# Splitting both plain up-projection weight groups early, and moving the norm's squares and its spreading into the first scheme stretch

## The chip, the cores and the metric

The kernel runs on one core of one Trainium2 chip. The metric is the device time of one execution in microseconds (us). Three runs of the kernel before took 1836.43, 1838.71 and 1839.90 us; the median is 1838.71 us. The engines are called as in the profile: PE multiplies matrices, DVE is the vector engine, ACT the engine of activations, POOL the general one, and SP issues most of the loads.

## What is computed

Two batches of tokens (512 and 256, held side by side as 768 columns) pass through two encoder layers with shared weights. The layers differ in their attention; both end in the same MLP, and this is where the change lies:

```python
for layer in range(DEPTH):
    ...
    h = rmsnorm(x, ln_mlp[layer])
    x = x + jnp.square(jax.nn.relu(h @ w_up[layer])) @ w_down[layer]
return rmsnorm(x, ln_f)
```

`w_up` is 1024 by 4096, `w_down` 4096 by 1024. The root of the mean square is one number for each token, so it can be multiplied in after the up-projection: the kernel multiplies `x` times the gain with `w_up` first and applies the factor `R` to the result.

## The kernel before

Activations lie transposed: eight tiles `x[k]` of 128 features by 768 tokens. Each fp32 operand of a product is cut into a rounded part (`whi`, `c` first half) and a remainder (`wlo`, `c` second half), and three matmuls stand for one exact one: hi·hi, hi·lo and lo·hi. ACT makes the rounded part by a copy, DVE the remainder by a subtraction. For a weight tile this is `wsplit` (lines 76 to 81): ACT's `whi<-wraw` at line 80 and DVE's `wlo<-wraw,whi` at line 81. There are three buffers for loaded weights (`wraw`), four each for `whi` and `wlo`.

The MLP of a layer (`mlp`, line 798) makes the up-projection in 16 stretches of 256 output columns, over two halves of the tokens (A and B, 384 each) and two halves of the features.

- The first two stretches are **plain**: four products of 24 matmuls each, 96 in all, from operands `c0` to `c3` that are ready when the attention's output projection ends. Each needs two weight tiles of 1024 columns, split whole.
- The other 14 are **scheme** stretches (`mp` from 2): seven products of 12 matmuls, 84 in all, of the kind of Strassen's and Winograd's. They need four more operands, `c4` to `c7`, and four weight tiles each: one loaded tile as it is (products 1 and 4), two tiles of sums `s` (6 and 5; 7 and 3), made by four POOL additions at line 866, and half a loaded tile (product 2). In the rows of an engine the products stand in the order 1, 3, 2, 6, 4, 7, 5.
- `second()` (line 822) makes `c4` to `c7`: for each of four pairs of feature tiles one ACT copy (line 828), four DVE combinations `t<-x,gains,t` (line 815), and for each of the four results an ACT copy and a DVE subtraction (`c<-t`, line 116, and `c<-t,c`, line 117).
- The norm: `nm.add(x[k])` (line 140) squares a tile on ACT (`sq<-x`, line 147) and adds it to `acc` on DVE (line 152). The squares share nine buffers with the eight tiles `x`, so one square is made, added and freed before the next. `nm.rstd()` sums `acc` over the partitions on PE (`ss`, line 161), then DVE (`ms`, line 164) and POOL (`rt`, line 166) make the factor; `nm.spread` copies it over all partitions on PE (`pb`, line 180) and DVE (`R<-pb`, line 182).
- `finish(z)` (line 893) applies relu and `R` on DVE (`z<-z,R`, line 894), squares on ACT (line 896) and writes the stretch to DRAM (`H<-z`, ACT's queue, line 898). The stretches' results `z` and the temporary `t` of `second()` share three buffers.

In the code before, the first plain stretch comes first, then `second()`, then all eight `nm.add`, then the second plain stretch with its loads and splits, then `rstd`, `spread` and `finish` of both, then the scheme stretches. A scheduler decides the final order on each engine: it moves instructions ahead of others of the same engine where it expects a gain, so the code's order is only its starting point. Within an engine the final order is fixed, and a waiting instruction holds up all that stand behind it.

Of the kernel before, what the change touches and what calls it, by code (L numbers as in the profile page):

```python
# [19 lines left out]
KD = D // P  # L20
# [17 lines left out]
def kernel(ctx: ExitStack, tc: tile.TileContext, a: dict, y: bass.AP):  # L38
# [22 lines left out]
    def ps_tile(tag, name):  # L61
        return psum.tile([P, 512], F32, tag=tag, name=name, bufs=BANKS[tag])
# [4 lines left out]
    def wload(src, width, pieces=1):  # L67

        off = woff.get(src, 0)
        woff[src] = off + P * width  # L70
        raw = wpool.tile([P, 1024], F32, tag="wraw", name="wraw", bufs=3)[:, :width]
        view = a[src][off : off + P * width].rearrange("(p w) -> p w", w=width)
        w = width // pieces
        return raw, [lambda s=slice(i * w, (i + 1) * w): nc.sync.dma_start(raw[:, s], view[:, s]) for i in range(pieces)]

    def wsplit(hi, lo, raw, dve=False):
        if dve:
            nc.vector.tensor_copy(hi, raw)
        else:
            nc.scalar.activation(hi, raw, AF.Copy)  # L80
        nc.vector.tensor_tensor(out=lo, in0=raw, in1=hi.bitcast(F32), op=ALU.subtract)  # L81

    def whilo(width):
        return (wpool.tile([P, 1024], F32R, tag="whi", name="whi", bufs=4)[:, :width],
                wpool.tile([P, 1024], F32R, tag="wlo", name="wlo", bufs=4)[:, :width])
# [43 lines left out]
    def gcol(g, k):  # L129
        return gains[:, g, k : k + 1]  # L130
# [667 lines left out]
    def mlp(layer, src, o, x, es):  # L798
# [7 lines left out]
        nm = Norm(sq)  # L806
# [3 lines left out]
        def put(pool, c, j, src, gain=None):  # L810
            t = comb[c, j] = pool.tile([P, 2, HT], F32R, tag=f"c{c}", name=f"c{c}", bufs=4)
            halve(t[:, 0], t[:, 1], src, gain)

        def stt(out, x_, s, y_, op):
            nc.vector.scalar_tensor_tensor(out=out, in0=x_, scalar=s, in1=y_, op0=ALU.mult, op1=op)
# [6 lines left out]
        def second():  # L822

            ts = []
            for j in range(4):
                xa, xb = x[j], x[j + 4]
                t = up.tile([P, 4, HT], F32, tag="z", name="t", bufs=3)
                nc.scalar.activation(t[:, 0], xa[:, A], AF.Copy, scale=gcol(g, j))
                stt(t[:, 1], xa[:, B], gcol(g, j), t[:, 0], ALU.subtract)
                stt(t[:, 2], xb[:, A], gcol(5 + layer, j + 4), t[:, 1], ALU.subtract)  # L830
                put(g2, 6, j, t[:, 2])
                stt(t[:, 3], xb[:, B], gcol(g, j + 4), t[:, 2], ALU.add)
                put(g2, 4, j, t[:, 3])
                stt(t[:, 0], xb[:, A], gcol(g, j + 4), t[:, 0], ALU.subtract)
                put(g2, 7, j, t[:, 0])
                put(g2, 5, j, t[:, 1])
# [6 lines left out]
        def weights(plain=False):  # L843


            raws = []
            for _ in range(2):
                raw, loads = wload("w_up", 1024)
                loads[0]()
                raws.append(raw)  # L850
            a11, a22, a12, a21 = (r[:, i * 512 : (i + 1) * 512] for r in raws for i in range(2))
            if plain:
                out = {}
                for t, ij in zip(raws, (((0, 0), (1, 1)), ((0, 1), (1, 0)))):
                    hi, lo = whilo(1024)
                    wsplit(hi, lo, t)
                    for i, b in enumerate(ij):
                        out[b] = (hi, lo), i * 512
                return out
            sa, sb = (up.tile([P, 1024], F32, tag="s", name="s", bufs=3) for _ in range(2))  # L860
            s2, s1, s3, s4 = (r[:, i * 512 : (i + 1) * 512] for r in (sa, sb) for i in range(2))
            out = {}
            for ps_, t in (((1, 4), raws[0]), ((6, 5), sa), ((7, 3), sb), ((2,), raws[1])):
                if t is sa:
                    for d_, x_, y_ in ((s1, a21, a22), (s2, s1, a11), (s3, a11, a21), (s4, a12, s2)):
                        nc.gpsimd.tensor_tensor(out=d_, in0=x_, in1=y_, op=ALU.add)  # L866
                w = 512 * len(ps_)
                hi, lo = whilo(w)
                wsplit(hi, lo, t[:, :w])
                for i, p in enumerate(ps_):  # L870
                    out[p] = (hi, lo), i * 512
            return out

        def product(ps, ws, cs):

            n = len(cs)
            for q, ((part, base), c) in enumerate(zip(ws, cs)):
                for k in range(4):
                    t = comb[c, k]
                    for i, (a_, b_) in enumerate(((0, 0), (0, 1), (1, 0))):  # L880
                        nc.tensor.matmul(ps, part[a_][:, base + k * P : base + (k + 1) * P], t[:, b_],  # L881
                                         start=q + k + i == 0, stop=q == n - 1 and k == 3 and i == 2)
            return ps

        def bank(n):
            return ps_tile("mm" if n in (6, 7, 3) else "at", "up")[:, :HT]

        def add(out, x_, y_, op=ALU.add):
            nc.vector.tensor_tensor(out=out, in0=x_, in1=y_, op=op)  # L889

        R, H, wait = [], [], []

        def finish(z):
            nc.vector.scalar_tensor_tensor(out=z, in0=z, scalar=0.0, in1=R[0][:, None, :].broadcast_to([P, 2, NT]),
                                           op0=ALU.max, op1=ALU.mult)
            nc.scalar.activation(z, z, AF.Square)
            H.append(dram.tile([P, 2, NT], F32, name=f"H{layer}_{len(H)}"))
            nc.scalar.dma_start(H[-1], z)

        def ztile():  # L900
            return up.tile([P, 4, HT], F32, tag="z", name="z", bufs=3).rearrange("p (i n) t -> p i (n t)", n=2)


        for fp in range(2):
            w = weights(True)
            z = ztile()
            for i in range(2):
                for n, (c, sl) in enumerate((((1, 2), B), ((0, 3), A))):
                    ps = product(bank(6 * n), [w[i, 0], w[i, 1]], c)
                    nc.scalar.activation(z[:, i, sl], ps, AF.Copy)  # L910
            wait.append(z)
            if fp == 0:
                second()
                for k in range(KD):
                    nm.add(x[k])
        R.append(nm.spread(nm.rstd()))
        while wait:
            finish(wait.pop(0))

        hs = []  # L920

        def read(pool, f):

            hr = pa_.tile([P, 2, NT], F32, tag="hr", name="hr", bufs=2)
            nc.gpsimd.dma_start(hr, H[f // 2])  # L925
            for i in range(2):
                hp = pool.tile([P, 2, NT], F32R, tag="hp", name="hp")
                halve(hp[:, 0], hp[:, 1], hr[:, i])
                hs.append((hp[:, 0], hp[:, 1]))

        for mp in range(2, FF // 256):
            w = weights()
            z = ztile()
            z12, z11, z22, z21 = z[:, 0, A], z[:, 0, B], z[:, 1, A], z[:, 1, B]
            one = lambda n: product(bank(n), [w[n]], [n])
            nc.scalar.activation(z11, one(1), AF.Copy)
            p3, p2 = one(3), one(2)
            if mp == FF // 256 - 1:

                g1s.close()  # L940
                pa_ = g1s.enter_context(tc.tile_pool(name=f"dna{layer}", bufs=4, reuse_waits="tile"))
                read(pa_, 0)
                read(pa_, 2)
            add(z12, one(6), z11)
            add(z11, p2, z11)
            p4 = one(4)
            add(z22, one(7), z12)
            add(z21, p4, z22, ALU.subtract)
            p5 = one(5)
            nc.vector.scalar_tensor_tensor(out=z22, in0=p5, scalar=-1.0, in1=z22, op0=ALU.mult, op1=ALU.subtract)  # L950
            add(z12, p5, z12)
            add(z12, p3, z12)
            finish(z)
        g2s.close()

# [33 lines left out]
    o, x, es = even_attention()  # L989
    es.close()  # L990
    hs_, xs, nm, spill = mlp(0, "w_out_e", o, x, hs_)
    sg = cpool.tile([P, 1], F32, name="sg")
    nc.scalar.dma_start(sg, a["subln"])
    nc.vector.tensor_scalar(sg, sg, 1.0 - LAM_INIT, None, op0=ALU.mult)
    o, x, es = odd_attention(xs, nm, sg, spill)
    es.close()
    mlp(1, "w_out_o", o, x, hs_)


# [129 lines left out]
```

## Time and profile before

| what | value |
|---|---|
| median of three runs | 1838.71 us (1836.43 to 1839.90) |
| span of the profiled execution, first to last instruction | 1832.9 us |
| PE busy | 1777.7 us (97%) |
| DVE, ACT, POOL busy | 1118.5, 764.7, 360.4 us |
| PE's matmuls of the up-projections (line 881), both layers | 2736 |
| up-projection of the first layer | from 373.4 us |
| up-projection of the second layer | from 1290.5 us |

The page gives no time of the profiled execution beyond its span; the median of the three runs is 5.8 us above that span, which is what lies around the first and the last instruction and the difference between executions. In a row of the timeline the columns are the start, the duration, the engine, the line, the operation, what it writes and reads, its shape and how many equal ones follow each other; in square brackets stand the idle time before it and what ended it. Durations of DVE rows contain some 0.08 us that overlap with the next row, so the distance of two starts is the better price.

### The profile page before, as it was taken

To read this page: it belongs to the slowest core of one execution; us is meant where nothing else is said; L and a number is where in the kernel's file an instruction comes from. 1 tells how busy PE (TensorE), PEld (TensorE's weight loads), DVE (VectorE), ACT (ScalarE), POOL (GpSimd) and SP (SyncE) were. 2 spreads that over 40 slices of the span, in tenths; PEclk is the share of its full clock that TensorE was granted. 3 is DMA by queue.
4 is the path that set the end of the run, shared out by engine and by line. 5 is a ranking of instruction groups with operands and counts; after the bars stand their busy time and mean duration, and the time that the engine had idled before them with its cause. 6 is when DMAs were issued, how large, how long until landed. Compare 5 with 4: busy or idle time off the path is not lost.

```text
span 1832.9 us, 28509 instructions
## 1 busy us (share of the span) xinstructions
PE 1777.7 (97%) x11358; PEld 1627.8 (89%) x11358; DVE 1118.5 (61%) x2083; ACT 764.7 (42%) x1485; POOL 360.4 (20%) x366
## 2 busy tenths in 40 slices
PE   7999999989999999999999999999799999999997
PEld 6878888879999988888999999988799999888877
DVE  7778646596666734325366776775956667343255
ACT  6665534353433412213235555554534334122143
POOL 2421000014544200000022222220145442000002
PEclk9999999989999999999999999999899999999999
DMA  5011223313333543323311110122133336433233
GB/s 176 32 33 47 66 74 111 106 35 110 121 135 124 198 136 127 127 69 114 99 48 46 47 47 21 53 67 92 35 104 126 136 123 197 136 127 127 70 99 114
DMA packets 50019, 176.70 MB, mean 96 GB/s; under 512 B 5856, under 2 KB 8672, under 8 KB 49888
## 3 DMA queue, kind: packets, MB, share of 16 engines
q1 hardware_dynamic: 38656, 121.91, 21.1%
q0 software_dynamic: 4608, 25.17, 4.1%
q10 hardware_dynamic: 6624, 27.81, 3.8%
q8 instruction: 89, 1.46, 0.3%
q14 instruction: 42, 0.34, 0.1%
HBM read 142.63 MB, written 31.46 MB: 95 GB/s over the span
## 4 chain that ended last, share of the span: by engine, by line
PE 79%; issue 7%; DVE 7%; DMA 3%; ACT 2%; POOL 1%; DVEq 0%; SPq 0%; ACTq 0%; POOLq 0%
PE up L881 25%; PE dna L204 11%; PE dqk L192 7%; PE dnb L204 6%; PE opa L204 5%; PE dvp L192 4%; PE fin L786 3%; PE opb L204 2%; DMA hr<-H 2%; PE npa L204 2%; PE ds L270 2%; PE dpv L713 2%; PE vp L192 1%; PE qp L192 1%; PE npv L598 1%
## 5 line engine op out<-in xcount | busy, mean ns | idle before, releaser
L881 PE MATMUL up<-c,whi 128*128 128x384 f32 x1824 | 469.5, 339 | 0.0
L881 PEld LDWEIGHTS up<-c,whi 128*128 128x128 f32 x1824 | 333.3, 190 | 0.1
L204 PE MATMUL dna<-hp,whi 128*128 128x512 f32 x896 | 331.5, 393 | 1.1 <-DVE hp L117 1.1
L80 ACT ACTIVATE whi<-wraw 128x1024 fp32r<-128x1024 f32 (+2 forms) x200 | 193.3, 967 | 325.2 <-PE dnb L204 223.8
L881 PE MATMUL up<-c,wlo 128*128 128x384 f32 x912 | 308.8, 340 | 17.8 <-DVE wlo L81 17.8
L81 DVE TENSOR_TENSOR wlo<-wraw,whi 128x1024 fp32r<-128x1024 f32 (+2 forms) x204 | 227.5, 1116 | 98.1 <-ACT whi L80 97.9
L204 PE MATMUL dnb<-hp,whi 128*128 128x256 f32 x896 | 250.3, 283 | 0.0
L204 PEld LDWEIGHTS dna<-hp,whi 128*128 128x128 f32 x896 | 168.0, 188 | 41.4 <-DVE hp L117 2.1
L881 PEld LDWEIGHTS up<-c,wlo 128*128 128x128 f32 x912 | 173.0, 190 | 18.5 <-DVE wlo L81 18.4
L866 POOL TENSOR_TENSOR s<-wraw 128x512 f32<-128x512 f32 x56 | 90.9, 1643 | 450.6 <-ACT c L116 217.3
L204 PE MATMUL dna<-hp,wlo 128*128 128x512 f32 x448 | 177.0, 395 | 0.0
L204 PEld LDWEIGHTS dnb<-hp,whi 128*128 128x128 f32 x896 | 167.2, 188 | 0.3
L889 DVE TENSOR_TENSOR z<-up,z 128x384 f32<-128x384 f32 x168 | 92.8, 552 | 105.5 <-PE up L881 103.7
L976 DVE TENSOR_TENSOR x<-dna,x 128x512 f32<-128x512 f32 x56 | 38.7, 691 | 166.1 <-PE dna L204 166.0
L204 PE MATMUL dnb<-hp,wlo 128*128 128x256 f32 x448 | 126.6, 283 | 0.0
L192 PE MATMUL dqk<-whi,xh 128*128 128x256 f32 x384 | 114.7, 299 | 0.0
L192 PE MATMUL dqk<-whi,xl 128*128 128x256 f32 x384 | 107.4, 280 | 0.0
L192 PE MATMUL dqk<-wlo,xh 128*128 128x256 f32 x384 | 107.2, 279 | 0.0
L925 POOL DMA_DIRECT2D hr<-H x32 | 17.5, 548 | 431.4 <-DVE hp L117 395.2
L204 PEld LDWEIGHTS dna<-hp,wlo 128*128 128x128 f32 x448 | 84.2, 188 | 18.7
L80 ACT ACTIVATE whi<-s 128x1024 fp32r<-128x1024 f32 x56 | 59.6, 1064 | 95.5 <-PE up L881 95.5
L698 ACT ACTIVATE de<-ds,m 128x512 f32<-128x512 f32 (+1 forms) x96 | 58.3, 612 | 81.1 <-DVE m L696 81.1
(214 smaller groups left out, 3870.2 us busy)
## 6 DMA issues: line engine op xcount, KB each, us to landing
wraw<-in_w_down_dram SPq DMA_DIRECT2D x72, 512.0 KB, 3.6
wraw<-in_w_up_dram SPq DMA_DIRECT2D x64, 512.0 KB, 3.5
H<-z ACTq DMA_DIRECT2D x32, 768.0 KB, 3.3
hr<-H POOLq DMA_DIRECT2D x32, 768.0 KB, 5.8
wraw<-in_w_in_o_dram SPq DMA_DIRECT2D x24, 512.0 KB, 3.6
wraw<-in_w_in_e_dram SPq DMA_DIRECT2D x16, 512.0 KB, 3.6
x<-in_xT_dram SPq DMA_DIRECT2D x16, 384.0 KB, 5.6
nbias<-in_bias_dram SPq DMA_DIRECT2D x20, 256.0 KB, 3.5
```

Source lines behind the costliest of these rows:

```text
L80: nc.scalar.activation(hi, raw, AF.Copy)
L81: nc.vector.tensor_tensor(out=lo, in0=raw, in1=hi.bitcast(F32), op=ALU.subtract)
L192: nc.tensor.matmul(ps[:, :256], st[:, tk], col(k, part, 0, 256), start=(k == 0 and i == 0), stop=(k == KD - 1 and i == 2))
L204: nc.tensor.matmul(ps[:, : e - s], w, mv[:, s:e], start=(k == 0 and i == 0), stop=(k == nk - 1 and i == 2))
L270: nc.tensor.matmul(out[h], q(a_, hp, qs), k(b_, hp, ks), start=i == 0, stop=i == 2)
L698: nc.scalar.activation(e, s, AF.Exp, bias=m, scale=1.0, accum_out=l2[:, c : c + 1])
L713: nc.tensor.matmul(pv, pt[:, i * P : (i + 1) * P], v[:, k0 // P + i, vc], start=(i == 0), stop=(i == nk - 1))
L786: nc.tensor.matmul(ps, lhs(k, part), mv[:, sl], start=(k == 0 and j == 0), stop=(k == GF - 1 and j == 2))
L866: nc.gpsimd.tensor_tensor(out=d_, in0=x_, in1=y_, op=ALU.add)
L881: nc.tensor.matmul(ps, part[a_][:, base + k * P : base + (k + 1) * P], t[:, b_], start=q + k + i == 0, stop=q == n - 1 and k == 3 and i == 2)
L889: nc.vector.tensor_tensor(out=out, in0=x_, in1=y_, op=op)
L976: evac_halves(pa, pb, lambda ps, s: nc.vector.tensor_tensor(out=xm[:, s], in0=ps, in1=xm[:, s], op=ALU.add))
```

## The change

Both plain stretches' weights are loaded and split ahead of everything else (`both`), the plain stretch itself becomes a function, and `second()` stands between the two. The norm's eight squares and additions move into the first scheme stretch (`mp == 2`), ahead of its first evacuation; `rstd` follows three products later, and `spread` and the `finish` of both plain stretches stand at the end of that stretch, directly ahead of its own `finish`. No instruction of arithmetic is added or removed.

```diff
-        for fp in range(2):
-            w = weights(True)
+        def plain(w):
             z = ztile()
             for i in range(2):
                 for n, (c, sl) in enumerate((((1, 2), B), ((0, 3), A))):
                     ps = product(bank(6 * n), [w[i, 0], w[i, 1]], c)
                     nc.scalar.activation(z[:, i, sl], ps, AF.Copy)
             wait.append(z)
-            if fp == 0:
-                second()
-                for k in range(KD):
-                    nm.add(x[k])
-        R.append(nm.spread(nm.rstd()))
-        while wait:
-            finish(wait.pop(0))
+
+        both = [weights(True) for _ in range(2)]
+        plain(both[0])
+        second()
+        plain(both[1])
...
             one = lambda n: product(bank(n), [w[n]], [n])
+            if mp == 2:
+                for k in range(KD):
+                    nm.add(x[k])
             nc.scalar.activation(z11, one(1), AF.Copy)
             p3, p2 = one(3), one(2)
+            if mp == 2:
+                rt = nm.rstd()
...
             add(z12, p3, z12)
+            if mp == 2:
+                R.append(nm.spread(rt))
+                while wait:
+                    finish(wait.pop(0))
             finish(z)
```

What the scheduler makes of it is seen in the order of instructions on the engines. First DVE in the first layer, where the operands of the plain stretches are complete (`c_4521` is the last of them), a minus for before and a plus for the change:

```order
 L120 SCALAR_TENSOR_TENSOR c_4521<-x_4319,gains,c_4521 128x384
-L152 TENSOR_TENSOR acc<-acc,sq 128x768
-L81 TENSOR_TENSOR wlo<-wraw,whi 128x1024
-L152 TENSOR_TENSOR acc<-acc,sq 128x768
+L81 TENSOR_TENSOR wlo<-wraw,whi 128x1024 x2
 L815 SCALAR_TENSOR_TENSOR t<-x_3718,gains,t 128x384
 L815 SCALAR_TENSOR_TENSOR t<-x_3916,gains,t 128x384
 L815 SCALAR_TENSOR_TENSOR t<-x_3832,gains,t 128x384 x3
```

The remainders of both tiles of the second plain stretch now stand ahead of `second()`; before, only the first of them did, and two additions of the norm beside it.

Second, DVE behind the last operand of `second()`. Before, in the first layer:

```order
L117 TENSOR_TENSOR c_4717<-t,c_4717 128x384
L152 TENSOR_TENSOR acc<-acc,sq 128x768
L81 TENSOR_TENSOR wlo<-wraw,whi 128x1024
L152 TENSOR_TENSOR acc<-acc,sq 128x768
L81 TENSOR_TENSOR wlo<-wraw,whi 128x1024
L152 TENSOR_TENSOR acc<-acc,sq 128x768
L81 TENSOR_TENSOR wlo<-s,whi 128x1024 x2
L164 TENSOR_SCALAR ms<-ss 128x6
L81 TENSOR_TENSOR wlo<-wraw,whi 128x512
```

With the change, in the first layer:

```order
L117 TENSOR_TENSOR c_4729<-t,c_4729 128x384
L81 TENSOR_TENSOR wlo<-wraw,whi 128x1024
L81 TENSOR_TENSOR wlo<-s,whi 128x1024
L152 TENSOR_TENSOR acc<-acc,sq 128x768 x4
L81 TENSOR_TENSOR wlo<-s,whi 128x1024
L152 TENSOR_TENSOR acc<-acc,sq 128x768
L81 TENSOR_TENSOR wlo<-wraw,whi 128x512
L152 TENSOR_TENSOR acc<-acc,sq 128x768
L164 TENSOR_SCALAR ms<-ss 128x6
```

With the change, in the second layer, from the last fifth of `second()` on:

```order
L81 TENSOR_TENSOR wlo<-s,whi 128x1024
L815 SCALAR_TENSOR_TENSOR t<-x_14064,gains,t 128x384 x3
L117 TENSOR_TENSOR c_14463<-t,c_14463 128x384
L117 TENSOR_TENSOR c_14471<-t,c_14471 128x384
L117 TENSOR_TENSOR c_14467<-t,c_14467 128x384
L117 TENSOR_TENSOR c_14474<-t,c_14474 128x384
L152 TENSOR_TENSOR acc<-acc,sq 128x768 x4
L81 TENSOR_TENSOR wlo<-s,whi 128x1024
L152 TENSOR_TENSOR acc<-acc,sq 128x768
L81 TENSOR_TENSOR wlo<-wraw,whi 128x512
L152 TENSOR_TENSOR acc<-acc,sq 128x768 x2
```

Before, the first `wlo<-wraw,whi` of the block belongs to the second plain stretch, and the second, the two of `s` and the half tile to the first scheme stretch. With the change all remainders of the block belong to the first scheme stretch: its first loaded tile, the sum tile of products 6 and 5, then four additions of the norm, and only then the sum tile of products 7 and 3. In the second layer the first two of these stand inside `second()`, and seven additions stand behind it, where the first layer has six.

Third, PE around the norm's two small groups in the first layer (`c_4383` is an operand of product 3, `c_4374` of product 1, `c_4664` of product 6, `c_4518` of product 2, `c_4729` of product 5). Before:

```order
L881 MATMUL up<-c_4521,wlo 128x384
L161 MATMUL ss<-ones,acc 128x2 x6
L881 MATMUL up<-c_4383,whi 128x384 x2
L881 MATMUL up<-c_4383,wlo 128x384
L180 MATMUL pb<-ident,rt 128x128 x6
L881 MATMUL up<-c_4374,whi 128x384 x2
```

With the change, around the sum:

```order
L881 MATMUL up<-c_4474,wlo 128x384
L881 MATMUL up<-c_4518,whi 128x384 x2
L881 MATMUL up<-c_4518,wlo 128x384
L161 MATMUL ss<-ones,acc 128x2 x6
L881 MATMUL up<-c_4664,whi 128x384 x2
```

And around the spreading:

```order
L881 MATMUL up<-c_4729,whi 128x384 x2
L881 MATMUL up<-c_4729,wlo 128x384
L180 MATMUL pb<-ident,rt 128x128 x6
L881 MATMUL up<-c_4374,whi 128x384 x2
L881 MATMUL up<-c_4374,wlo 128x384
```

Before, only three matmuls stood between the sum over the partitions and the spreading; now four whole products (6, 4, 7 and 5) do.

## Prediction

> **What bounds the kernel now.** I read the page first, then PE's waits, then the timeline of the two places where it waits longest, and last the chain behind them.
>
> ```profile
> span 1832.9 us, 28509 instructions
> PE 1777.7 (97%) x11358; PEld 1627.8 (89%) x11358; DVE 1118.5 (61%) x2083; ACT 764.7 (42%) x1485; POOL 360.4 (20%) x366
> ```
>
> PE is busy 97% of the span, so a change that leaves the matmuls as they are can win only what is left: idle time, and time in which matmuls run slowly. PE's list of waits says where the idle time is.
>
> ```profile
> PE up L881 <- DVE wlo L81: 17.8, 2, 9.4
> PE pb L180 <- POOL rt L166: 4.3, 4, 1.4
> ```
>
> 17.8 us lie in two waits, one in each layer's up-projection, and some more in front of the norm's spreading. The timeline of PE shows both places, first layer and then second.
>
> ```profile
> 373.44 0.51 PE L881 MATMUL up<-c,whi 128*128 128x384 f32 x2
> 373.79 0.34 PE L881 MATMUL up<-c,wlo 128*128 128x384 f32 x1
> ...
> 404.54 0.69 PE L881 MATMUL up<-c,wlo 128*128 128x384 f32 x1 [8.41 <-DVE wlo L81]
> 405.03 0.84 PE L881 MATMUL up<-c,whi 128*128 128x384 f32 x2
> ...
> 408.23 0.58 PE L881 MATMUL up<-c,whi 128*128 128x384 f32 x2
> ...
> 421.07 2.11 PE L180 MATMUL pb<-ident,rt 128*128 128x128 f32 x12 [1.42 <-POOL rt L166]
> 422.83 0.99 PE L881 MATMUL up<-c,whi 128*128 128x384 f32 x2
> ...
> 425.66 0.51 PE L881 MATMUL up<-c,whi 128*128 128x384 f32 x2
> ...
> 1290.46 0.51 PE L881 MATMUL up<-c,whi 128*128 128x384 f32 x2
> ...
> 1322.52 0.69 PE L881 MATMUL up<-c,wlo 128*128 128x384 f32 x1 [9.38 <-DVE wlo L81]
> ...
> 1326.72 0.34 PE L881 MATMUL up<-c,wlo 128*128 128x384 f32 x1
> ...
> 1339.15 1.60 PE L180 MATMUL pb<-ident,rt 128*128 128x128 f32 x12 [1.43 <-POOL rt L166]
> ```
>
> Two starts from 373.44 to 373.79 give 0.175 us for a matmul. After the wait it is slower: 11 matmuls stand between 404.54 and 408.23, which is 3.69 us instead of 1.93. The window of the wait shows why.
>
> ```profile
> 396.20:404.50 8.30, 0.00 (x0) 0.00 (x0) 8.30 (x16) 4.72 (x9) 0.00 (x0) 0.62 0.00 0
> ```
>
> The last but two columns are the granted clock: 0.62 in the idle stretch, and DVE's 8.30 us say that DVE was busy throughout. The chain shows with what.
>
> ```profile
> 384.26 2.95 DVE c L117 x2
> 387.21 3.67 DVE t L815 x3
> 390.88 1.88 DVE c L117 x4
> ...
> 393.29 0.87 DVE acc L152
> 394.15 1.59 DVE t L815 x3
> ...
> 403.35 1.15 DVE wlo L81
> ```
>
> DVE makes the scheme's operands and the norm's sums, and the remainder that the second plain stretch needs comes last. PE waits for an order, not for work.
>
> **What the change removes.** The order on the engines shows both remainders of the second plain stretch ahead of `second()`. DVE had the end of the plain operands some 4 us after PE's start and needs 1.15 us for each, so they are there by about 380, and PE asks for them at 373.44 + 96·0.175 = 390.2. That wait goes, with the slow matmuls behind it: 8.41 + 1.76 us in the first layer; in the second 9.38 us and 13 matmuls from 1322.52 to 1326.72, 4.20 us instead of 2.28, so 1.92. The wait for `rt` goes too, since four products (8.4 us) now stand between sum and spreading, where DVE and POOL needed 3.3 us: 1.42 us and 9 slow matmuls from 422.83 to 425.66 (2.83 instead of 1.58, so 1.25) in the first layer, 1.43 in the second. **Removed: 12.84 + 12.73 = 25.6 us.** The small matmuls of sum and spreading stay as many as they were.
>
> **What it adds: a wait at product 3.** The first scheme stretch begins 192 matmuls after the start, product 3 is the second in PE's rows, and it needs the sum tile of products 7 and 3. On DVE this remainder now stands behind `second()`, the loaded tile, the other sum tile and four additions of the norm, and the additions go at the pace of squares that share one free buffer:
>
> ```profile
> 402.40 0.95 DVE L152 TENSOR_TENSOR acc<-acc,sq 128x768 f32<-128x768 f32 x1
> ...
> 404.41 0.95 DVE L152 TENSOR_TENSOR acc<-acc,sq 128x768 f32<-128x768 f32 x1
> ...
> 406.41 0.94 DVE L152 TENSOR_TENSOR acc<-acc,sq 128x768 f32<-128x768 f32 x1
> ```
>
> One addition each 2.0 us. First layer: before, `second()` ended at 402.40 with two additions in it; now one is in it, so 402.40 − 0.87 = 401.5. Two remainders: 403.8. Additions start at 403.8, 405.8, 407.8 and 409.8; ACT ends the fourth square at 409.8, then rounds the sum tile (1.06 us); the remainder ends at 410.8 + 1.2 = 412.0. PE is at product 3 after 204 matmuls, at 409.1, and after two rounded ones, at 409.5, it wants the remainder: a wait of 2.5 us. Second layer: `second()` ended at 1320.39, two additions leave it and two remainders enter it, so 1320.39 − 1.74 + 2.3 = 1320.95, the sum tile is ready 8.2 us later at 1329.15, PE is there at 1290.46 + 35.7 + 0.35 = 1326.5: 2.6 us.
>
> ```profile
> 1320.39 0.94 DVE L152 TENSOR_TENSOR acc<-acc,sq 128x768 f32<-128x768 f32 x1
> ```
>
> **And POOL stretches DVE there.** Beside POOL's additions DVE's small operations take 1.2 to 1.5 us instead of 0.5 (384.26 and 387.21 in the chain: five in 6.6 us instead of 2.5).
>
> ```profile
> 383.85 2.94 POOL L866 TENSOR_TENSOR s<-wraw 128x512 f32<-128x512 f32 x2 [191.18 <-ACT c L116]
> 386.76 1.60 POOL L866 TENSOR_TENSOR s<-s,wraw 128x512 f32<-128x512 f32 x1
> 388.44 1.50 POOL L866 TENSOR_TENSOR s<-wraw,s 128x512 f32<-128x512 f32 x1
> ...
> 410.94 2.54 POOL L866 TENSOR_TENSOR s<-wraw 128x512 f32<-128x512 f32 x2 [21.01 <-DMA wraw<-in_w_up_dram]
> ```
>
> ```profile
> 405.28 1.21 DVE L81 TENSOR_TENSOR wlo<-wraw,whi 128x1024 fp32r<-128x1024 f32 x1
> ```
>
> The next stretch's additions begin 4.5 us after the first loaded tile's remainder (ending 406.4) frees a buffer. Now this remainder ends at 402.7, so POOL runs from 407.2 to about 412.5: over the third and fourth addition and the remainder, 0.8 us each as the rows above have it, 2.3 us. In the second layer it ends at 1312.4 within `second()`, POOL runs from 1317 on over operations that follow each other without a gap, and the whole 4.1 us is lost. **Waits at product 3: 2.5 + 2.3 = 4.8 and 2.6 + 4.1 = 6.7 us**, from 2.5 and 2.6 without POOL to 6.6 and 7.8 with its four operations in full. The page SBUF — State Buffer of the Trainium skill (section Who interferes with whom) says that a DVE instruction with two SBUF inputs and a GpSimd one that reads SBUF exclude each other, so that the later one blocks fully. By that the second layer would lose POOL's 5.2 us (four operations of 1.3) and the time would come out 1.1 us later; the rows above, 4.1 us for the five, agree in kind.
>
> Slow matmuls follow again: rows have 1.76 and 1.92 us behind waits of 8 to 9 us, 1.25 us behind the spreading in the first layer and none in the second, so 0 to 1.9; I take 1.3 and 1.6. The page TensorE: Matmul & The Clock Gate (Part 1) has the clock halved only after an idle window of about 3.4 us; the 0.62 row agrees, and by that waits of 2.5 us would cost no slow matmul.
>
> **What it moves to the third and fourth scheme blocks.** Three `finish` now follow each other on DVE, and the second scheme stretch's `z` needs the buffer of the first plain one.
>
> ```profile
> 422.35 0.69 DVE L182 COPY R<-pb 128x512 f32<-128x512 f32 x1 [2.53 <-PE pb L180]
> 423.21 0.42 DVE L182 COPY R<-pb 128x256 f32<-128x256 f32 x1 [0.17 <-PE pb L180]
> 423.67 3.43 DVE L894 SCALAR_TENSOR_TENSOR z<-z,R 128x1536 f32<-128x1536 f32 x2
> ...
> 432.24 1.15 DVE L889 TENSOR_TENSOR z<-up,z 128x384 f32<-128x384 f32 x2 [5.14 <-PE up L881]
> ```
>
> ```profile
> 426.78 1.47 ACT L896 ACTIVATE z<-z 128x1536 f32<-128x1536 f32 x1
> ```
>
> ```profile
> H<-z ACTq DMA_DIRECT2D x32, 768.0 KB, 3.3
> ```
>
> Count from the end X of product 2. The sum (1.25) and four products reach X + 9.7, the spreading X + 11.5, and PE ends the second scheme stretch at X + 26.2. DVE has the first copy of `R` at X + 11.7, an addition, the second copy and the last half remainder at X + 13.4, or 15.8 if POOL stretches the three remainders there by 0.8 each. The first `finish` takes 1.7 more, its square 1.5, its write 3.3: X + 19.9 to 22.3. ACT's evacuation of product 1 (0.5) waits for that; behind it on ACT stand the next rounded weights, on DVE three additions (0.55 each; the third waits for product 7 at X + 24.1 in any case) and the third scheme stretch's first remainder. It is ready at X + 25.8, or 27.4 if the write beside two others takes 5 us; PE wants it at X + 26.5. That is 0 to 0.9 us, and up to 3 if POOL's additions stretch DVE once more. I take 1.0 for each layer. PE itself goes on meanwhile, since its banks are free.
>
> **The sum.** 25.6 − (4.8 + 6.7) − (1.3 + 1.6) − 2.0 = 9.2 us won. Against the profiled execution 1832.9 − 9.2 = 1823.7 us of span; with the 5.8 us by which the median of the runs stands above it, 1838.7 − 9.2 = **1829.5 us**.
>
> **The rivals.**
>
> 1. *The new wait is short*: the additions and POOL slip past each other, product 3 costs 2.5 and 2.6 us and no slow matmul. For it speaks that DVE has gaps between the additions. 25.6 − 5.1 = 20.5 us, 1818.2 us. Against it: in the second layer there are no gaps where POOL falls.
> 2. *The wait only moves*: 6.6 and 7.8 us at product 3, 1.9 us of slow matmuls each and 3.0 us in the third scheme stretch: 24.2 us, 1.4 won, 1837.3 us. For it speaks that every bound here is one that a row has shown; against, that all must come together.
> 3. *Slower, by the writes of three `finish`*: the write of 3.3 us in the row stood beside one other; now three of 768 KB stand together with weight loads. With POOL's stretching PE's wait grows one for one once the write takes over 4.1 us from issue to landing. At 11.6 us it is 7.5 us in each layer instead of 1, which eats the 9.2 us and 3.8 more; at 13 us the time is 1845 us. Against it: three such writes at the row's rate take 9.9 us in all, and the one that matters is the first.
> 4. *The change doesn't do what it says*, and PE waits in the second plain stretch as before: 1838.7 us. The order on DVE speaks against it, with 10 us to spare.
>
> **How the numbers follow.** The forecast gets 0.56, the short wait 0.24, the moved wait 0.13, slower 0.05, no effect 0.02. The range goes from the short wait, 1818, to near the moved one, 1836; what is left out is most of rivals 2 to 4. About 0.2% (3.7 us) is what a measurement of this kernel can tell from no change: faster 0.80 (forecast and first rival), same 0.15 (moved wait, no effect), slower 0.05.
>
> **What would show it.** PE's waits for `wlo` in the plain stretches are gone, and two new ones stand some 35 us after the start of each up-projection, in front of product 3, near 5 and 7 us, the second longer. The granted clock dips behind them. The wait for `rt` is below 0.1 us in both layers. POOL's second group of additions starts near 407 and 1317. In the third scheme stretch PE waits at most 3 us. Wrong would be: no wait at product 3 at all, or one over 8 us, or a wait in the third scheme stretch that ends with a write of `H`.

## The result, and the profile after

The changed kernel takes 1821.84 us (median of four runs, 1820.18 to 1824.15), the kernel before 1837.57 us (four runs, 1836.23 to 1839.90). The ratio is 0.9915 with a 95% interval of 0.9901 to 0.9929, so 13.0 to 18.2 us are won. The prediction was 1829.5 us in a range of 1818 to 1836, with 9.2 us won.

The page of the changed kernel, and from PE's list of waits the rows of the up-projection and the spreading:

```profile
span 1820.1 us, 28502 instructions
PE 1777.1 (98%) x11358; PEld 1627.3 (89%) x11358; DVE 1127.7 (62%) x2083; ACT 764.2 (42%) x1485; POOL 363.5 (20%) x366
```

```profile
PE up L881 <- ACT whi L80: 5.8, 2, 5.1
...
PE up L881 <- DVE wlo L81: 2.1, 2, 1.7
...
PE pb L180 <- POOL rt L166: 1.5, 2, 1.0
```

The 17.8 us of the plain stretches are gone; 7.9 us stand in four short waits instead, and two of the four waits for `rt` have left the list. PE's timeline shows where the new ones are, first layer and then second:

```profile
375.07 0.51 PE L881 MATMUL up<-c,whi 128*128 128x384 f32 x2
...
411.76 0.62 PE L881 MATMUL up<-c,whi 128*128 128x384 f32 x2 [0.72 <-ACT whi L80]
414.12 0.69 PE L881 MATMUL up<-c,wlo 128*128 128x384 f32 x1 [1.74 <-DVE wlo L81]
...
419.43 1.40 PE L161 MATMUL ss<-ones,acc 128*128 128x2 f32 x12
...
429.11 1.50 PE L180 MATMUL pb<-ident,rt 128*128 128x128 f32 x12
...
1283.75 0.51 PE L881 MATMUL up<-c,whi 128*128 128x384 f32 x2
...
1324.92 0.94 PE L881 MATMUL up<-c,whi 128*128 128x384 f32 x2 [5.11 <-ACT whi L80]
1326.18 0.69 PE L881 MATMUL up<-c,wlo 128*128 128x384 f32 x1 [0.32 <-DVE wlo L81]
...
1331.17 1.40 PE L161 MATMUL ss<-ones,acc 128*128 128x2 f32 x12
```

From 375.07 to 411.04, where the wait begins, PE runs its 204 matmuls without a pause. Then product 3 waits 0.72 + 1.74 = 2.46 us in the first layer and 5.11 + 0.32 = 5.43 in the second. Behind the waits the 22 matmuls up to the sum take 5.31 and 4.99 us instead of 22·0.175 = 3.85, and the two ahead of the remainder 0.62 and 0.94 instead of 0.35: 1.7 us of slow matmuls in each layer. The spreading (429.11) starts without a wait.

DVE in the second layer shows what the remainder of product 3 (the `wlo<-s` at 1324.90) stands behind:

```profile
1310.66 4.79 DVE L815 SCALAR_TENSOR_TENSOR t<-x,gains,t 128x384 f32<-128x384 f32 x3
1315.38 3.07 DVE L117 TENSOR_TENSOR c<-t,c 128x384 fp32r<-128x384 f32 x4
1318.36 0.95 DVE L152 TENSOR_TENSOR acc<-acc,sq 128x768 f32<-128x768 f32 x1
...
1323.95 0.96 DVE L152 TENSOR_TENSOR acc<-acc,sq 128x768 f32<-128x768 f32 x1 [0.91 <-ACT sq L147]
1324.90 1.23 DVE L81 TENSOR_TENSOR wlo<-s,whi 128x1024 fp32r<-128x1024 f32 x1
```

Four additions, one each 1.87 us, and ahead of them the end of `second()`, stretched: that is the order the prediction had read.

### The profile page after: what moved, and what is told of

It reads as the page before. It is cut to its first block, busy times and chain, and to the rows that moved or that the text cites. A ratio compares the mean times of both kernels' runs of the same rounds, so it can differ in the third digit from the quotient of the medians.

```text
span 1820.1 us, 28502 instructions
## 1 busy us (share of the span) xinstructions
PE 1777.1 (98%) x11358; PEld 1627.3 (89%) x11358; DVE 1127.7 (62%) x2083; ACT 764.2 (42%) x1485; POOL 363.5 (20%) x366
## 3 DMA queue, kind: packets, MB, share of 16 engines
q1 hardware_dynamic: 38656, 121.91, 21.2%
## 4 chain that ended last, share of the span: by engine, by line
PE 78%; DVE 8%; issue 8%; DMA 3%; ACT 3%; POOL 1%; DVEq 0%; SPq 0%; ACTq 0%; POOLq 0%
PE up L881 23%; PE dna L204 11%; PE dqk L192 8%; PE dnb L204 6%; PE opa L204 5%; PE dvp L192 4%; PE fin L786 3%; DMA hr<-H 2%; PE opb L204 2%; PE npa L204 2%; PE ds L270 2%; PE dpv L713 2%; DVE t L815 1%; PE vp L192 1%; PE qp L192 1%
## 5 line engine op out<-in xcount | busy, mean ns | idle before, releaser
L116 ACT ACTIVATE hp<-hr 128x768 fp32r<-128x768 f32 x64 | 50.9, 837 | 100.2 <-PE dnb L204 61.8
```

The source lines that it names most:

```text
L116: nc.scalar.activation(hi, src, AF.Copy)
```

## The experiments

Every kernel was timed beside runs of the kernel before on the same chip (medians 1836.92 to 1839.34 us there), so ratios are compared. The changed kernel's is 0.9915 (0.9901 to 0.9929).

| kernel | median, us | ratio to before | interval |
|---|---|---|---|
| split alone | 1831.93 | 0.9972 | 0.9962 to 0.9982 |
| norm's move alone | 1820.45 | 0.9917 | 0.9903 to 0.9931 |
| split, sum and spreading moved, additions not | 1819.60 | 0.9897 | 0.9880 to 0.9913 |
| changed, without POOL's sums of the second scheme stretch | 1817.34 | 0.9886 | 0.9871 to 0.9901 |
| changed, two buffers for sum tiles | 1819.56 | 0.9911 | 0.9896 to 0.9926 |
| changed, two buffers for squares | 1826.07 | 0.9937 | 0.9924 to 0.9949 |
| changed, products 1, 6, 4, 5, 3, 7, 2 | 1827.44 | 0.9942 | 0.9929 to 0.9954 |
| changed, product 6 ahead of 3 | 1817.35 | 0.9893 | 0.9880 to 0.9907 |
| same, and two buffers for sum tiles | 1818.37 | 0.9897 | 0.9883 to 0.9911 |
| same (product 6 ahead), first scheme weights preferred | 1820.07 | 0.9902 | 0.9885 to 0.9918 |
| additions not moved, product 6 ahead of 3 | 1817.01 | 0.9884 | 0.9869 to 0.9898 |

### The change in parts: the split alone

```diff
         plain(both[0])
         second()
+        for k in range(KD):
+            nm.add(x[k])
         plain(both[1])
+        R.append(nm.spread(nm.rstd()))
+        while wait:
+            finish(wait.pop(0))
```

The three blocks for `mp == 2` are taken out; the diff is against the changed kernel.

> Half of the change: both plain weight groups are loaded and split ahead, but the norm's squares and additions, its sum and its spreading stay where they were (between and behind the plain stretches). Theory O (it is DVE's order that makes PE wait, and the change earns by taking the norm's additions out of the way of the first sum): the waits for wlo of the plain stretches go (21.5 us with their slow matmuls), but the sum over the partitions now stands in the last product of the second plain stretch, some 33 us after the start, while six additions and three remainders still follow second() on DVE; PE waits at the sum for acc, about 6 us in the first layer and 9 in the second, and again 2 us for rt. About 1832 to 1836 us, 10 us or more above the changed kernel (1821.8). Rival S (the early split is what earns, the norm's move is worth only the wait for rt): 1.4 us for rt in each layer and some slow matmuls, so 1825 to 1827 us.

Measured: 0.9972, some 5 us won and no more. The time was nearly that of theory O (1831.93 us against 1832 to 1836), its reason was not. PE's timeline in the first layer:

```profile
412.10 0.62 PE L881 MATMUL up<-c,whi 128*128 128x384 f32 x2 [2.52 <-ACT whi L80]
414.44 0.69 PE L881 MATMUL up<-c,wlo 128*128 128x384 f32 x1 [1.72 <-DVE wlo L81]
...
416.39 2.72 PE L161 MATMUL ss<-ones,acc 128*128 128x2 f32 x12 [0.30 <-DVE acc L152]
...
420.78 2.93 PE L180 MATMUL pb<-ident,rt 128*128 128x128 f32 x12
```

The scheduler had put product 3 ahead of product 1, with sum and spreading inside it, so PE waited there and hardly at the sum. The waits, 4.5 us here and 4.3 in the second layer, are only 0.9 us longer in all than the changed kernel's 7.9. The rest shows in the windows of the same kernel, whose last but two column is the granted clock:

```profile
416.00:418.00 2.00, 1.70 (x9) 1.61 (x8) 2.00 (x2) 0.00 (x0) 1.46 (x1) 0.50 0.00 0
...
422.00:424.00 2.00, 2.00 (x11) 2.00 (x10) 0.94 (x2) 0.00 (x0) 0.00 (x0) 0.50 0.00 0
424.00:426.00 2.00, 2.00 (x12) 2.00 (x11) 1.97 (x3) 0.00 (x0) 0.00 (x0) 0.87 0.00 0
```

The clock stays at half for 10.2 us, though PE is busy 2.00 of 2.00 us from 418 on; in the second layer for 13.7, two of them within waits. That costs about 5 and 6 us, where the changed kernel loses 1.7 in each layer.

### The norm's move alone

```diff
-        both = [weights(True) for _ in range(2)]
-        plain(both[0])
+        plain(weights(True))
         second()
-        plain(both[1])
+        plain(weights(True))
```

> The other half: the norm's squares, sum, spreading and the finish of the plain stretches are moved into the first scheme stretch as in the change, but in the code the second group of weights is loaded and split only after second(). Theory O: as soon as the additions are gone from the code between the plain stretches, the scheduler puts both remainders ahead of second() by itself; the order on DVE and PE is that of the change, so the time is that of the changed kernel, 1821.8 within 0.2% (1818 to 1826). Rival S: the early split in the code earns the 21.5 us of the plain waits and this kernel lacks it: it wins only the rt wait, 4.1 us less than before, 1833 us or more.

Measured: 0.9917, the changed kernel's time. The waits are those of the changed kernel (5.75 us in two for `whi`, 2.2 for `wlo`). Rival S falls: the early split in the code is not needed once the norm is out of the way. But the kernel with the split alone has no wait in its plain stretches either. Either edit brings both remainders ahead; the difference lies in the norm's move, and the next kernel shows in which part of it.

### Sum and spreading moved, additions not

```diff
+        for k in range(KD):
+            nm.add(x[k])
         plain(both[1])
...
-            if mp == 2:
-                for k in range(KD):
-                    nm.add(x[k])
```

> The changed kernel with the norm's eight squares and additions back between the plain stretches; the sum, the spreading and the three finish stay in the first scheme stretch. The order on DVE up to the factor is that of the kernel with the split alone (1831.9 us), the order on PE is that of the changed kernel, so it tells apart why the split alone was so much slower. Theory H (there the 24 small matmuls of sum and spreading stood in the stretch of half clock behind the wait, which lasted 10 us instead of 3 for it): with these matmuls gone from there the half-clock stretch is 3 us again, product 3 stands one product later than it did, and the waits are about 2 us in each layer: 1816 to 1820 us. Rival N (it was the additions: between the remainders they make the first sums late by as much as the change won): waits of 4 us or more in each layer as in the kernel with the split alone, 1827 us or more.

Measured: 0.9897, against 0.9972 with the split alone, although DVE's order is the same up to the factor. Product 3 waited 0.42 + 1.74 us in the first layer (product 2 another 0.27) and 0.62 + 2.76 in the second, and the windows of the first layer show the half clock ending after 3.4 us:

```profile
416.00:418.00 2.00, 2.00 (x9) 2.00 (x8) 2.00 (x2) 0.00 (x0) 1.92 (x2) 0.59 0.00 0
418.00:420.00 2.00, 1.73 (x7) 1.23 (x6) 0.90 (x1) 0.00 (x0) 0.35 (x1) 0.56 0.08 12
420.00:422.00 2.00, 2.00 (x17) 2.00 (x15) 0.00 (x0) 0.80 (x1) 0.00 (x0) 1.00 0.68 250
```

In the second layer it lasted over six. Theory H holds: moving the 24 small matmuls out of the slow stretch, with product 1 ahead of product 3, is what the split alone lacked. In the traces the two up-projections are together 9.2 us shorter than with the split alone: some 3 us of it are shorter waits (5.8 us instead of 8.8) and some 6 us fewer slow matmuls. How much of the latter the small matmuls make, and how much the new order of the products, these two runs do not separate. Moving the additions as well wins nothing that this measurement shows (0.9897 and 0.9915, overlapping).

### POOL's part in the wait that is left

First POOL's additions of the second scheme stretch were left out, and their tiles filled with a constant:

```diff
-                        nc.gpsimd.tensor_tensor(out=d_, in0=x_, in1=y_, op=ALU.add)
+                        if mp == 3:
+                            nc.gpsimd.memset(d_, 0.5)
+                        else:
+                            nc.gpsimd.tensor_tensor(out=d_, in0=x_, in1=y_, op=ALU.add)
...
-            w = weights()
+            w = weights(False, mp)
```

> The changed kernel without POOL's additions for the second scheme stretch: the four sums of that stretch's weights are left out and their tiles filled with a constant, in both layers, so that POOL reads nothing from SBUF while DVE works through the end of second() and the norm's additions. Theory P (POOL's additions stretch DVE, and in the second layer that is most of the wait at product 3): the three combinations of 4.79 us and four remainders of 3.07 us in the second layer take 2.5 to 3 and 2 us, the remainder of 2.30 us in the first layer 1.2; the waits at product 3 fall from 2.46 and 5.43 us to about 1.4 and 2, and with the slow matmuls behind them 4 to 6 us go: 1816 to 1818. Rival Q (the pace of the squares' one free buffer sets the wait, POOL's part is slack): waits as in the changed kernel and a time within 0.1% of 1821.8.

Measured: 0.9886. DVE's rows of the second layer without POOL, the same operations as the first two rows above:

```profile
1308.69 1.67 DVE L815 SCALAR_TENSOR_TENSOR t<-x,gains,t 128x384 f32<-128x384 f32 x3
1310.28 1.96 DVE L117 TENSOR_TENSOR c<-t,c 128x384 fp32r<-128x384 f32 x4
```

4.79 became 1.67 and 3.07 became 1.96: 4.2 us. The waits fell to 0.61 + 0.64 and 0.89 + 0.65 us. In the second layer POOL makes most of the wait, as theory P has it; in the first layer half of it, by the one remainder that took 2.30 us and now 1.23.

Then two of the four additions were held back by a buffer, with nothing left out:

```diff
-            sa, sb = (up.tile([P, 1024], F32, tag="s", name="s", bufs=3) for _ in range(2))
+            sa, sb = (up.tile([P, 1024], F32, tag="s", name="s", bufs=2) for _ in range(2))
```

> The changed kernel with two buffers for the tiles of weight sums instead of three, the order on every engine being the same. POOL can then make the second tile of the second scheme stretch only after the remainder of product 3 has read the buffer, so that two of its four additions leave the window in which DVE is late. Theory P (POOL's additions stretch DVE): about half of the 4.2 us by which DVE's rows grew in the second layer goes, the wait there falls from 5.43 to about 3.3, in the first from 2.46 to about 2: 2 to 3 us less, 1818.5 to 1820 us. Rival W (the sums of the second scheme stretch are now late themselves): PE waits for whi or wlo of a sum in that stretch, or in a later one in each of the 14, and the time is 1823 us or more.

Measured: 0.9911. The waits at product 3 fell to 0.69 + 0.66 and 2.95 + 0.65 us, as theory P has it, but the two additions that were held back now stretched the norm's last ones, and in the second layer the sum waited:

```profile
1326.38 1.50 PE L161 MATMUL ss<-ones,acc 128*128 128x2 f32 x12 [0.72 <-DVE acc L152]
```

The 2 us that the trace gains do not stand out from the interval.

### The pace of the squares

```diff
-        nm = Norm(sq)
+        nm = Norm(lambda: sq() if nm.n % 2 else cpool.tile([P, NT], F32, tag="R", name="sqr", bufs=1))
```

> The changed kernel with two free buffers for the norm's squares instead of one (every other square goes to the tile that later holds R). Theory B (the additions go at 1.87 us because one square must be added and freed before the next is made): they now follow each other at 0.9 to 1.1 us. But the order on DVE changes with it: all six (first layer) and seven (second) additions that are left stand ahead of the remainder of product 3's tile, before it was four; 6 times 1.0 instead of 4 times 1.87 us is 1.5 us earlier in the first layer, 7 times 1.0 is 0.5 us earlier in the second. So the waits at product 3 become about 1 and 5 us, and the time 1819 to 1821 us. Rival A (the pace is set by ACT, which makes the squares between its other work): the additions stay at 1.9 us, six or seven of them take 11 to 13 us, product 3 waits 6 us or more in the first layer and 10 in the second, and the time is 1829 us or more.

Every other square now goes to the tile that later holds `R`. Measured: 0.9937, by the median slower than the changed kernel (the intervals overlap slightly), and nothing won. DVE in the first layer:

```profile
403.94 0.96 DVE L152 TENSOR_TENSOR acc<-acc,sq 128x768 f32<-128x768 f32 x1
405.00 0.96 DVE L152 TENSOR_TENSOR acc<-acc,sqr 128x768 f32<-128x768 f32 x1
406.07 1.87 DVE L152 TENSOR_TENSOR acc<-acc,sq 128x768 f32<-128x768 f32 x1
408.04 1.87 DVE L152 TENSOR_TENSOR acc<-acc,sqr 128x768 f32<-128x768 f32 x1
```

Theory B was right on the pace, 1.06 us from start to start. But POOL works from 405.71 on, and additions without gaps take twice as long beside it. The waits became 0.84 + 3.68 and 5.53 + 0.43 us. Theory B's time had left POOL out.

### Product 3 later

```diff
+            if mp == 2:
+                p4, p6, p5 = one(4), one(6), one(5)
+                p3 = one(3)
+                rt = nm.rstd()
+                p7, p2 = one(7), one(2)
...
```

> The changed kernel with another order of the products in the first scheme stretch alone: products 1, 6, 4, 5, then 3 (the one that waits), 7, 2, and the norm's sum behind product 3; nothing else is changed. Theory L (what is left of the loss is that product 3 comes too early: its remainder is late by 2.46 and 5.43 us, and the other tile of sums has long been split): product 3 is wanted 6.3 us later, both waits and the slow matmuls behind them go (4.4 and 7.3 us of delay), and the time falls to 1810 to 1813 us. Rival M (the wait only moves: to the sum, which needs all eight additions, or to the spreading, which has two products instead of four between it and the sum, or to evacuations that now come together on DVE): new waits of 3 us or more in each layer, 1816 us or more.

Measured: 0.9942; rival M holds. The list of waits has nothing left at product 3, and this instead:

```profile
PE pb L180 <- POOL rt L166: 9.6, 4, 4.4
...
PE ss L161 <- DVE acc L152: 4.1, 2, 2.6
```

POOL's timeline says why two products between sum and spreading do not cover the chain here:

```profile
423.50 1.29 POOL L866 TENSOR_TENSOR s<-wraw 128x512 f32<-128x512 f32 x1 [8.00 <-DMA wraw<-in_w_up_dram]
424.87 2.14 POOL L866 TENSOR_TENSOR s<-s,wraw 128x512 f32<-128x512 f32 x1
426.95 1.27 POOL L866 TENSOR_TENSOR s<-wraw 128x512 f32<-128x512 f32 x1
428.17 1.34 POOL L166 TENSOR_TENSOR rt<-ms,nhalf 128x6 f32<-128x6 f32 x1
```

DVE had `ms` at 421.45, but the factor stood behind three additions that themselves waited for a load. Moving one product alone avoids this:

```diff
+            p6 = one(6) if mp == 2 else None
             p3, p2 = one(3), one(2)
...
-            add(z12, one(6), z11)
+            add(z12, p6 or one(6), z11)
```

> The changed kernel with one product moved in the first scheme stretch alone: product 6 stands ahead of product 3, so the order is 1, 6, 3, 2, sum, 4, 7, 5, and three products instead of four stand between the norm's sum and its spreading. Theory L (product 3 comes too early for its remainder): it is wanted 2.1 us later, so the wait falls from 2.46 to 0.4 us in the first layer and from 5.43 to 3.3 in the second, and the slow matmuls behind the first go (1.7 us): 4 to 6 us less than the changed kernel, 1816 to 1818 us. Rival M (the time goes into the spreading again, as with the larger reordering, where it waited over 4 us with two products between): three products take 6.3 us, and on DVE two evacuations stand ahead of the factor; a wait for rt of 2 us or more in each layer and a time of 1821 us or more.

Measured: 0.9893. The waits are 0.62 us in the first layer, where no slow matmuls follow, and 3.00 + 0.25 in the second; at the spreading there is none. Theory L holds, by the waits; the interval of the time (0.9880 to 0.9907) still overlaps the changed kernel's.

### Combinations

Product 6 first, and two buffers for sum tiles:

> Both of these edits together: product 6 ahead of product 3 in the first scheme stretch, and two buffers for the tiles of weight sums. If both theories hold, the waits at product 3 are about 0 and 1.2 us and the slow matmuls behind them mostly gone: 1813 to 1816 us. If either rival holds, a new wait stands at the spreading (for rt) or at a sum's weights in a scheme stretch, and the time is 1819 us or more.

0.9897, no better than with product 6 alone. Product 3 waits 0 and 0.86 + 0.64 us, but the sum waits 1.80 us for the last addition in the second layer: the same shift as above.

Product 6 first, and the weights of the first scheme stretch preferred:

```diff
-            w = weights()
+            with tc.high_priority() if mp == 2 else ExitStack():
+                w = weights()
```

> The kernel with product 6 ahead of product 3 (1817.35 us), with the weights of the first scheme stretch preferred by the scheduler: on DVE the remainders of its loaded tile and of its first sum tile stand within second(), and three additions instead of four stand ahead of the remainder of product 3. Theory O (DVE's order alone makes the wait): one addition of 1.87 us less ahead of it takes the second layer's wait from 3.25 to about 1.4 us and the first layer's 0.6 to 0; with the slow matmuls 3 to 4 us less, 1813.5 to 1815 us. Rival P (POOL's additions begin when the loaded tile's remainder frees its buffer, which now comes some 5 us earlier, within second(), so they stretch DVE's combinations in both layers): nothing is won, 1816.5 us or more.

0.9902. Rival P holds: POOL began at 398.29 within `second()`, three combinations took 3.74 us instead of 1.67, and product 3 waited 2.4 and 2.7 us.

Product 6 first, and the additions back between the plain stretches:

> Additions back between the plain stretches, and product 6 ahead of product 3. If theory H and theory L both hold, the waits at product 3 are below 0.5 us in each layer and no slow matmuls follow: 1812 to 1815 us. If the additions make the sums late (rival N) product 3 still waits 2 us or more in each layer, or the sum waits for the last addition: 1817 us or more.

0.9884, interval 0.9869 to 0.9898, below the changed kernel's from end to end. It is the lowest ratio of a version that computes everything, but its interval overlaps those of the others with product 6 ahead of 3. Four waits of 0.37 to 1.51 us are left at products 3 and 2, and the granted clock stays at 1.00 through both up-projections. The best case that was expected, waits below 0.5 us and 1812 to 1815 us, did not come.

## Why the prediction was right, and by how much it was off

**The removal (25.6 us) held.** No wait is left in the plain stretches, and none at the spreading.

**The new wait at product 3 was in the right place, behind the right queue, and too large: 2.46 and 5.43 us instead of 4.8 and 6.7.** The two terms of that sum were 2.5 and 2.6 us without POOL, and 2.3 and 4.1 us of POOL's stretching. The kernel without POOL's sums measures them: its waits are 1.25 and 1.54 us, so POOL added 1.2 and 3.9.

The term without POOL was too large by 1.2 and 1.1 us. An addition takes 1.87 us and not 2.0, which is 0.4 us over three of them, and `second()` ended up to 0.3 us sooner. The rest lies in the count: PE waited first for the rounded part of the sum tile and ran the two rounded matmuls within the stretch, where the prediction had them ahead of the wait.

POOL's term was right in the second layer. POOL began at 1309.27, 25.5 us after the start of the up-projection instead of 26.5, over operations without gaps, and DVE's rows grew by 4.2 us, not by the 5.2 of a full exclusion. In the first layer the term was mis-sized: 2.3 us over the third and fourth addition and the remainder (three times 0.8 is 2.4). POOL did begin where the prediction said:

```profile
407.73 3.30 POOL L866 TENSOR_TENSOR s<-wraw 128x512 f32<-128x512 f32 x2 [15.52 <-DMA wraw<-in_w_up_dram]
410.99 1.99 POOL L866 TENSOR_TENSOR s<-s,wraw 128x512 f32<-128x512 f32 x1
```

```profile
408.81 1.06 DVE L152 TENSOR_TENSOR acc<-acc,sq 128x768 f32<-128x768 f32 x1 [0.91 <-ACT sq L147]
410.79 1.05 DVE L152 TENSOR_TENSOR acc<-acc,sq 128x768 f32<-128x768 f32 x1 [0.91 <-ACT sq L147]
411.77 2.30 DVE L81 TENSOR_TENSOR wlo<-s,whi 128x1024 fp32r<-128x1024 f32 x1
```

The additions stood 1.87 and 1.98 us apart beside it: they have 0.91 us of idle time between them, and that took POOL's share. Only the remainder grew, from 1.23 to 2.30 us. That the gaps would absorb POOL is what the first rival, the short wait, had said. Its 2.5 us for the first layer met the 2.46 by luck, though: half of them were POOL's after all, and slow matmuls followed, which it had ruled out.

**Slow matmuls: 1.7 us in each layer instead of 1.3 and 1.6.** What the prediction took from the Trainium skill (TensorE: Matmul & The Clock Gate, Part 1), by which waits of 2.5 us would cost none, does not fit: behind 0.72 + 1.74 us the clock was 0.50.

```profile
414.00:416.00 2.00, 1.88 (x6) 1.88 (x7) 2.00 (x3) 0.00 (x0) 1.20 (x1) 0.50 0.00 0
```

The 0.62 row, which the prediction read as agreeing, does not bear out an idle time of 3.4 us either: 8.30 us with a mean of 0.62 are 2.0 us at full clock and 6.3 at half, so the clock fell 2.0 us after PE stopped. The last section shows on what it hangs. That the two estimates came so near was partly luck: the kernel with the norm's move alone has the waits of the changed kernel, and its half clock lasted 0 and 6.8 us instead of 3.4 and 3.4.

**The third scheme stretch: nothing instead of 1.0 us in each layer.** Counted from the end of product 2 (X, 419.43), the rows are

```profile
433.33 5.08 DVE L894 SCALAR_TENSOR_TENSOR z<-z,R 128x1536 f32<-128x1536 f32 x3
...
443.69 1.22 DVE L81 TENSOR_TENSOR wlo<-wraw,whi 128x1024 fp32r<-128x1024 f32 x1
```

```profile
440.62 0.49 ACT L936 ACTIVATE z<-up 128x384 f32<-128x384 f32 x1 [0.46 <-DMA H<-z]
```

The first `finish` starts at X + 13.9, the write has landed when ACT goes on at X + 21.2, and the remainder is ready at X + 25.5, within an us of when PE wants it (X + 26.5). The chain was right; the middle of its range was taken, and the remainder came 0.3 us ahead of the lower end (X + 25.8).

**The sum.** 25.6 − 7.9 (waits) − 3.4 (slow matmuls) = 14.3 us, against 9.2 forecast: 3.6 from the waits, 2.0 from the third stretch, less 0.5 for slow matmuls. The medians give 15.7, with the interval from 13.0. Between the first and the last matmul of an up-projection the two traces have 255.4 and 254.9 us before, 246.0 and 249.0 after: 15.3 us less. The spans differ by 12.8 only, because the rest of the trace, which the edit leaves alone, is 2.5 us longer. Of the 5.8 us between span and median before, only 2.0 us lie around a span (1822.1 − 1820.1 in the changed kernel's profiled run), so the profiled execution of before was itself a short one.

The rival of the `H` writes was not tried by itself. No wait of PE for them stands in the changed kernel's third scheme stretch, and the three writes took 3.6 us from issue to landing at the median, far from the 11.6 us at which the win would have been lost. Why the clock stays at half while the small matmuls run was not taken apart.

## What to carry to other kernels

When an engine waits for an order and not for work, find what stands behind the moved work on each in-order queue, and price the next wait: here 25.6 us went and 11.3 came back a stretch later. Small matmuls are not harmless because they are few: keep them out of the stretch behind a wait, and leave enough work between a sum and its use to cover the queues of all engines in the chain. A gap between dependent operations can absorb the cost of a neighbouring engine that stretches them; closing the gap brings that cost out.

## What the runs showed of the hardware that was not expected

- The granted clock changes in steps. In all 13 traces its changes lie, within 0.01 us, on one grid of 3.41 us in each execution, and the half-clock stretches of the up-projections last one to four steps: 3.4, 6.8, 10.2 or 13.7 us. A half-clock step in which PE has work throughout costs half of it, 1.7 us.
- Short waits are enough for the half clock, and it hangs on how they fall on that grid. These are single steps:

| kernel | step, us | PE busy in it, us | clock in the next step |
|---|---|---|---|
| before | 394.69 to 398.11 | 1.44 | 0.50 |
| changed | 410.25 to 413.66 | 1.41 | 0.50 |
| changed | 1318.20 to 1321.61 | 1.61 | 1.00 |
| without POOL's sums | 1317.23 to 1320.64 | 1.88 | 0.50 |
| norm's move alone | 410.96 to 414.37 | 1.96 | 1.00 |
| norm's move alone | 407.54 to 410.96 | 2.46 | 1.00 |
| product 6 ahead, two buffers for sum tiles | 1324.26 to 1327.67 | 2.26, the sum's 12 matmuls among them | 0.50 |

The changed kernel's waits of 0.72 + 1.74 us fell into one step; almost the same waits (0.65 + 1.76 us) of the norm's move alone fell into two, and no half clock followed. A sharp bound does not come out of the traces (1.61 and 1.88 us), and in the last row a step with small matmuls was followed by half clock with more of it busy. Without POOL's sums 0.61 + 0.64 us left the clock at 1.00 in the first layer, and 0.89 + 0.65 us in the second brought it to 0.50 for one step:

```profile
414.00:416.00 2.00, 2.00 (x12) 2.00 (x12) 1.69 (x3) 1.66 (x4) 0.00 (x0) 1.00 0.00 0
```

```profile
1322.00:1324.00 2.00, 2.00 (x8) 2.00 (x7) 1.09 (x2) 0.91 (x2) 0.00 (x0) 0.50 0.75 229
```

- With the 24 small matmuls in that stretch it lasted 10.2 and 13.7 us, though PE was idle for only 0.4 and 2.1 us of it.
- POOL's additions doubled DVE's (0.96 to 1.87 us) when these had no gaps. With a constant written by POOL instead, DVE's rows were as short as alone. The page SBUF — State Buffer of the Trainium skill (Who interferes with whom) says as much of a GpSimd instruction that only writes.
